# Token tiles ahead of the modulation weights, and a first h made on two engines, at the start of a one-layer diffusion step

## The chip, the cores and the metric

The kernel runs on 1 core of one Trainium2 chip. The metric is the device time of one execution in microseconds (us). In the text PE is TensorE (its matmuls; PEld is its weight loads), DVE is VectorE, ACT is ScalarE, POOL is GpSimd, and SP is SyncE, whose queue issues most DMAs.

## The reference

One trunk layer works on 128 prompt tokens and 1024 sample tokens of width 1024. Cut to what matters here:

```python
shift, scale, gate = modulation(cond, w_mod, b_mod)        # silu(cond) @ w_mod + b_mod, in thirds
h = rmsnorm(x, norm_gain) * (1.0 + scale) + shift           # cond is c_ctx for the prompt, c for the sample
q_a, k_a, v_a, g_a, q_b, k_b, v_b, g_b = split(h @ w_in)    # w_in: 1024 x 2560
# q, k: RMSNorm by head, rotary positions on sample tokens
o_a = global attention of mixer A;  o_b = windowed attention of mixer B with a sink
x = x + gate * (concat(o_a * silu(g_a), o_b * silu(g_b)) @ w_out)
```

The outputs are both new x and the prompt's k and v of both mixers. All is in float32.

## The kernel before, in words

The tokens are 9 tiles of 128 rows: tile 0 is the prompt, tiles 1 to 8 the sample. The width is cut into 8 chunks of 128 (`KT`). A product in float32 is made of three products in a shorter format: each operand is split in a high part (`h_at(0, ...)`, `whi`) and a low part (`h_at(1, ...)`, `wlo`), and high x high, high x low and low x high are summed in PSUM.

The change lies wholly in the first stage, which makes h and, beside it, the gate projection of mixer A (`W_GA`). For each chunk j:

- `load_wm(j)` loads the modulation weights of the chunk (1 MB). `modulate_rows(j)` multiplies them with the conditioning on PE into PSUM tile `pm` and copies the rows out (`mrows`). `modulate(j)` turns these rows on PE, back into `pm`, and DVE sums them (`m4`) into the columns `a_mod` and `b_col`: factor and addend of this chunk.
- `load_x(t)` loads token tile t into `xn`. `norm(t)` takes its sum of squares on ACT, the mean and the power -0.5 on POOL (`msx`, `rsx`), and `scaled` multiplies the tile on DVE.
- `transposed(j, t0, n, cond)` turns n token tiles' chunk j on PE into PSUM tile `px`. ACT makes `hf` = a x px + b from it, DVE casts hf to the high part of h, and POOL subtracts to get the low part.
- `W_GA.split()` makes the high part of the next chunk's weights on ACT and the low part on DVE, and loads one more chunk into one of three buffers `raw`.
- `first_gates` and `next_gates` are the products: `big` for tiles 1 to 4 (512 columns), `small` for tiles 5 and 6 (256 columns), one chunk later.

In pass j of the loop the products of chunk j - 1 run while chunk j is modulated and turned. Passes 0 and 1 have no steady work yet. PE is kept at work there by `warm(n)`: n products of the identity (`ident_b`) into a bank that is overwritten later; their counts stand in `WARM`.

The tiles of PSUM named `pm` and `px` take two banks in turns (`bank_tr`). Each engine executes its instructions in the order of the code, since `in_order` ties them; only semaphores make it wait. The DMAs of SP are issued in that order too, into one queue.

Of the kernel before, what the change touches and what calls it, by code (L numbers as in the profile page):

```python
# [9 lines left out]
F32 = mybir.dt.float32  # L10
F32R = mybir.dt.float32r
BF16 = mybir.dt.bfloat16
AF = mybir.ActivationFunctionType
ALU = mybir.AluOpType
# [4 lines left out]
P = 128  # L19
D = 1024  # L20
KT = D // P
# [34 lines left out]
PAD = 2  # L56
X_FROM = 1
SECOND_FROM = 5
WARM = (8, 4, 4, 2)
WIDE = 5  # L60
LOADLEAD = 5
OUTRATE = 2.5
PADRATE = 3
POOL_LO = ("gb",)
NOG = 5
PES = 3
GATE_LATE = 2
# [40 lines left out]
def hybrid_step(ctx, tc, x_prompt, x_sample, cache_k_a, cache_v_a, cache_k_b, cache_v_b,  # L108
# [3 lines left out]
    nc = tc.nc  # L112
    x_tile = [x_prompt[0]] + [x_sample[0, P * i : P * i + P, :] for i in range(NL)]
# [28 lines left out]
    def bank(tag, name):  # L142
        return ps.tile([P, 512], F32, tag=tag, name=name, bufs=BANKS[tag])
# [5 lines left out]
    def bank_tr(name):  # L149
        turn["tr"] += 1  # L150
        return bank("DE"[turn["tr"] % 2], name)
# [33 lines left out]
    def h_at(lo, i, k, to):  # L185
        c = k - k % GROUP[i]
        return h_tile[lo, i, c][:, k - c, to]


    def third(ts):  # L190

        for i, (a, b) in enumerate(THIRDS):
            if a <= ts.start and ts.stop <= b:
                return i, slice(ts.start - a, ts.stop - a)
# [4 lines left out]
    a_mod = sm.tile([P, KT, 2], F32, name="a_mod")  # L199
    b_col = sm.tile([P, KT, 2], F32, name="b_col")  # L200
# [5 lines left out]
    class Weights:  # L206
# [22 lines left out]
        def split(self):  # L229
            k = len(self.hi)  # L230
            h = wp.tile([P, 512], F32R, tag="whi", name=f"whi{self.tag}_{k}")
            l = wp.tile([P, 512], F32R, tag="wlo", name=f"wlo{self.tag}_{k}")
            nc.scalar.copy(h, self.raw[k])
            eng = nc.gpsimd if self.tag in POOL_LO and k % 2 else nc.vector
            eng.tensor_tensor(l, self.raw[k], h, op=ALU.subtract)
            self.hi.append(h)
            self.lo.append(l)
            self.load()
# [3 lines left out]
    W_GA = Weights([(CG[0], 512)], "ga")  # L242
# [67 lines left out]
    FIRST = [1, 2, 3, 4, 5, 6]  # L310
    with tc.tile_pool(name="st", bufs=2, side="right") as st:
        ident = st.tile([P, P], F32, name="ident", bufs=1)
# [8 lines left out]
        def group_sum(out, eye):  # L321
            nc.vector.tensor_tensor(out, eye[:, 0:2], eye[:, 32:34], op=ALU.add)
            for a in (64, 96):
                nc.vector.tensor_tensor(out, out, eye[:, a : a + 2], op=ALU.add)

        wm = []

        def load_wm(j):
            w = st.tile([P, KT, 2, P], F32, tag="wm", name=f"wm{j}", bufs=3)
            nc.sync.dma_start(w, w_mod_ss[j])  # L330
            wm.append(w)

        load_wm(0)
        nc.scalar.activation(silc, colt[:, 0:16], AF.Silu)
        bsc1 = st.tile([P, 8], F32, name="bsc1", bufs=1)
        st.tile([P, 24], F32, name="pad4", bufs=1)
# [9 lines left out]
        def modulate_rows(j):  # L346
            pm = pmod[j] = bank_tr(f"pm{j}")
            for k in range(KT):
                a = 32 * (k % 4)
                nc.tensor.matmul(pm[a : a + 32, 0:256], sil32[:, k, :], wm[j][:, k].rearrange("p s n -> p (s n)"),  # L350
                                 start=(k < 4), stop=(k >= 4), tile_position=(0, a))
            mrows[j] = st.tile([P, 256], F32, tag="mrows", name=f"mrows{j}")
            (nc.scalar.copy if j else nc.vector.tensor_copy)(mrows[j], pm[:, 0:256])
# [10 lines left out]
                                    op0=ALU.add, op1=ALU.mult)  # L364
            nc.vector.tensor_scalar(b_col[:, j, :], m4[:, 1], colt[:, 24 + j : 25 + j], None, op0=ALU.add)

        xn = {}

        def load_x(t):
            xn[t] = st.tile([P, D], F32, name=f"xn{t}", bufs=1)  # L370
            nc.sync.dma_start(xn[t], x_tile[t])

        rx = {}

        def scaled(t, r):
            nc.vector.tensor_scalar(xn[t], xn[t], r, None, op0=ALU.mult)

        def norm(t, now_=True):
            xm = xn[t]
            sq = st.tile([P, D], BF16, tag="sq", name=f"sq{t}", bufs=1)  # L380
            ss = st.tile([P, 1], F32, tag="ss", name=f"ss{t}")
            nc.scalar.activation(sq, xm, AF.Square, accum_out=ss)
            ms = st.tile([P, 1], F32, tag="ms", name=f"msx{t}")
            nc.gpsimd.tensor_scalar(ms, ss, 1.0 / D, EPS, op0=ALU.mult, op1=ALU.add)
            r = st.tile([P, 1], F32, tag="rs", name=f"rsx{t}")
            nc.gpsimd.tensor_tensor(r, ms, mhalf[:, 0:1], op=ALU.pow)
            if now_:
                scaled(t, r)
            else:
                rx[t] = r  # L390

        def transposed(j, t0, n, cond):
            px = bank_tr(f"px{j}_{t0}")
            for i in range(n):
                if j == 0 and t0 == 1:
                    warm(WARM[3])
                nc.tensor.transpose(px[:, P * i : P * i + P], xn[t0 + i][:, P * j : P * j + P], ident)
            w = P * n
            dst = slice(P * place(t0), P * place(t0) + w)
            hf = st.tile([P, 512], F32, tag="hf", name=f"hf{j}_{t0}", bufs=3)  # L400
            nc.scalar.activation(hf[:, :w], px[:, :w], AF.Identity,
                                 scale=a_mod[:, j, cond : cond + 1], bias=b_col[:, j, cond : cond + 1])
            step = w if third(dst) else 2 * P
            for o in range(0, w, step):
                i, to = third(slice(dst.start + o, dst.start + o + step))
                nc.vector.tensor_copy(h_at(0, i, j, to), hf[:, o : o + step])
                nc.gpsimd.tensor_tensor(h_at(1, i, j, to), hf[:, o : o + step], h_at(0, i, j, to), op=ALU.subtract)

        for t in FIRST[:4]:
            load_x(t)  # L410
        W_GA.load()
        load_x(5)
        load_x(6)
        load_wm(1)
        W_GA.load()
        load_wm(2)
        def warm(n):

            for _ in range(n):
                nc.tensor.matmul(small[0], ident_b, ident_b.unsqueeze(1).to_broadcast([P, 4, P]), start=True, stop=True)  # L420
# [19 lines left out]

        for j in range(KT + 2):
            if j == 0:
                warm(WARM[0])
                norm(1)
                modulate_rows(0)
                warm(WARM[1])
                norm(2)
                modulate(0)
                warm(WARM[2])
                norm(3)  # L450
                norm(4)
                W_GA.split()
                norm(5)
                transposed(0, 1, 4, 0)
                norm(6)
                load_wm(3)
                continue
            big_on, small_on = j <= KT, 2 <= j
            if j < KT:
                W_GA.split()  # L460
            if big_on:
                first_gates(0, j - 1, 0)
                first_gates(1, j - 1, 0)
            if j < KT:
                modulate_rows(j)
                if j + 3 < KT:
                    load_wm(j + 3)
                if X_FROM <= j < X_FROM + 3:
                    load_x(rest[j - X_FROM])
            if big_on:  # L470
                first_gates(0, j - 1, 1)
                first_gates(1, j - 1, 1)
            if j == 1:
                transposed(0, 5, 2, 0)
            if big_on:
                first_gates(2, j - 1)
            if j < KT:
                modulate(j)
                transposed(j, 1, 4, 0)
            if big_on:  # L480
                first_gates(3, j - 1)
            if j < KT:
                transposed(j, 5, 2 if j < WIDE else 4, 0)
            if X_FROM + 1 < j <= X_FROM + 4:
                t = rest[j - X_FROM - 2]
                scaled(t, rx.pop(t))
            if X_FROM < j <= X_FROM + 3:
                norm(rest[j - X_FROM - 1], False)
            for ch in range(4):
                if small_on:  # L490
                    next_gates(ch, j - 2)
                if ch % 2 or j >= KT:
                    more()
            if KT - 2 <= j < KT:
                raw = st.tile([P, KT, 2, P], F32, tag="wm", name=f"raw_qa{j}", bufs=3).rearrange(
                    "p (k a) s n -> p k (a s n)", a=2)
                k0 = 4 * (j - KT + 2)
                c0, n = W_QA.cols[0]
                nc.sync.dma_start(
                    raw, w_in[P * k0 : P * k0 + 512, c0 : c0 + n].rearrange("(k p) n -> p k n", p=P))  # L500
                W_QA.raw += [raw[:, k] for k in range(4)]
# [49 lines left out]
    with tc.tile_pool(name="qt", bufs=2, side="right") as qt:  # L551
# [90 lines left out]
        for m in range(2):  # L642
            w, nxt = ((W_QA, W_QB), (W_QB, W_KV))[m]
            ts = list(range(1, NT)) + [0]
            for t in ts:
# [3 lines left out]
                if (m, t) in ((0, ts[-2]), (1, ts[GATE_AT[0]])):  # L649
                    n = len(wg) // 2  # L650
# [390 lines left out]
    for f in beside[2]:  # L1041
# [5 lines left out]
        name=nc.get_next_instruction_name(), engine=mybir.EngineType.Activation, act_func_set_id=6))  # L1047
# [63 lines left out]
    def values(i, b, last, blk, ph, pl):  # L1111
# [36 lines left out]
        def parts():  # L1148
            while held[0] == NOG:
                outq.pop(0)()  # L1150
# [172 lines left out]
```

## Time and profile before

| | |
|---|---|
| time of 3 runs | 723.15, 723.17, 726.25 us; median 723.17 |
| span of the profiled execution, first to last instruction | 721.3 us |
| mean granted clock of PE over the span | 0.993 |
| busy in the span | PE 97%, DVE 63%, ACT 57%, POOL 46% |
| first real product (first_gates of chunk 0) | starts at 17.47 us |
| modulation products of chunks 1, 2, 3 (`pm`) | start at 18.59, 26.42, 32.72 us |

Of the profiled execution the span is what is known; its own time is not shown apart from it. A row of the timeline gives start, duration, engine, line, operation and tiles (output <- inputs), and in brackets how long the engine stood idle before it and what ended that. Buffer numbers are left out there, so `xn` is any token tile. The granted clock is the share of full speed at which PE may run.

### The profile page before, as it was taken

To read this page: it belongs to the slowest core of one execution; us is meant where nothing else is said; L and a number is where in the kernel's file an instruction comes from. 1 tells how busy PE (TensorE), PEld (TensorE's weight loads), DVE (VectorE), ACT (ScalarE), POOL (GpSimd) and SP (SyncE) were. 2 spreads that over 40 slices of the span, in tenths; PEclk is the share of its full clock that TensorE was granted. 3 is DMA by queue.
4 is the path that set the end of the run, shared out by engine and by line. 5 is a ranking of instruction groups with operands and counts; after the bars stand their busy time and mean duration, and the time that the engine had idled before them with its cause. 6 is when DMAs were issued, how large, how long until landed. Compare 5 with 4: busy or idle time off the path is not lost. (4 is left out here: it accounts for less than half of the span.)

```text
span 721.3 us, 10622 instructions
## 1 busy us (share of the span) xinstructions
PE 698.3 (97%) x3524; PEld 559.7 (78%) x3524; DVE 457.6 (63%) x1007; ACT 411.7 (57%) x829; POOL 335.3 (46%) x355
## 2 busy tenths in 40 slices
PE   5999999999999999999999999999999999999997
PEld 2678988877777788977788888888888888887865
DVE  3466147875675872745866677577666775775653
ACT  5355411411232451158778877877787778877770
POOL 3456013332322340236666555655575557555751
PEclk9999999999999999999999999999999999999999
DMA  8961373348435115440321222121212221212323
GB/s 344 346 219 59 121 278 86 79 94 276 121 85 142 45 60 171 139 143 23 103 67 45 73 67 88 44 81 52 87 54 59 66 87 45 81 53 87 103 65 119
DMA packets 53159, 78.56 MB, mean 109 GB/s; under 512 B 6569, under 2 KB 25449, under 8 KB 52081
## 3 DMA queue, kind: packets, MB, share of 16 engines
q1 hardware_dynamic: 44928, 65.96, 28.1%
q10 hardware_dynamic: 8176, 11.94, 6.3%
q8 instruction: 28, 0.46, 0.3%
q14 instruction: 27, 0.21, 0.1%
HBM read 58.69 MB, written 19.18 MB: 108 GB/s over the span
## 5 line engine op out<-in xcount | busy, mean ns | idle before, releaser
L1108 POOL TENSOR_TENSOR pl<-pe,ph 128x512 fp32r<-128x512 f32 x130 | 167.6, 1292 | 144.7 <-DVE nm L919 67.5
L859 DVE TENSOR_REDUCE mx<-pmx 128x1 f32<-128x384 f32 x192 | 101.4, 552 | 59.5 <-PE pmx L858 58.1
L1100 ACT ACTIVATE pe<-st 128x512 f32<-128x512 f32 x146 | 86.8, 594 | 28.0 <-PE st L1098 27.1
L1104 ACT CAST ph<-pe 128x512 fp32r<-128x512 f32 x146 | 90.6, 621 | 4.8
L1118 PE MATMUL pv<-ph,v_hi 128*128 128x512 f32 x208 | 83.2, 400 | 2.2 <-DVE spare L1142 2.2
L1121 PE MATMUL pv<-pl,v_hi 128*128 128x512 f32 x208 | 82.6, 397 | 0.0
L173 POOL TENSOR_TENSOR rs_q<-ms_q,mhalf 128x8 f32<-128x8 f32 x18 | 34.8, 1931 | 82.1 <-DVE ms_q L171 82.1
L1189 PE MATMUL po<-wo,ogh 128*128 128x512 f32 x216 | 72.5, 394 | 0.2 <-DVE yt L1196 0.2
L919 DVE CUSTOM_DVE_ANT_0 sn<-sn,mask,nsink 128x512 f32<-128x512 f32 (+1 forms) x64 | 46.3, 724 | 38.3 <-PE sn L916 36.5
L858 PE MATMUL pmx<-kha,qt 128*128 128x384 f32 x192 | 61.0, 363 | 0.4 <-ACT pen L905 0.2
L1097 PE MATMUL st<-qt,kha 128*128 128x512 f32 x144 | 58.3, 405 | 1.5 <-ACT pe L1100 0.8
L1098 PE MATMUL st<-qb,kla 68*128 68x512 f32 x144 | 57.6, 400 | 1.1 <-DVE qb L878 1.1
L1120 PE MATMUL pv<-ph,v_lo 128*64 128x512 f32 x146 | 57.9, 396 | 0.0
L1121 PEld LDWEIGHTS pv<-pl,v_hi 128*128 128x128 f32 x208 | 39.4, 189 | 16.7 <-issue 0.2
L905 ACT ACTIVATE pen<-sn,nm 128x512 f32<-128x512 f32 (+2 forms) x72 | 45.0, 626 | 6.5 <-DVE nm L919 3.1
L1093 ACT CAST ph<-st 128x512 fp32r<-128x512 f32 x62 | 36.4, 587 | 19.9 <-PE st L1092 18.7
L1118 PEld LDWEIGHTS pv<-ph,v_hi 128*128 128x128 f32 x208 | 39.4, 189 | 10.5 <-ACT ogh L1154 2.4
L1189 PEld LDWEIGHTS po<-wo,ogh 128*128 128x128 f32 x216 | 40.0, 188 | 6.8 <-DVE yt L1196 0.6
L1094 DVE TENSOR_TENSOR pl<-st,ph 128x512 fp32r<-128x512 f32 x62 | 42.5, 686 | 2.3 <-ACT ph L1093 1.5
L1189 PE MATMUL po<-wo,ogl 128*128 128x512 f32 x108 | 42.6, 394 | 0.0
L594 ACT ACTIVATE sqq<-pq 128x512 f32<-128x512 f32 x18 | 10.8, 599 | 53.3 <-DMA qd<-qo0q 14.4
L858 PEld LDWEIGHTS pmx<-kha,qt 128*128 128x128 f32 x192 | 35.5, 190 | 6.2 <-DVE mx L859 1.4
(216 smaller groups left out, 1700.2 us busy)
## 6 DMA issues: line engine op xcount, KB each, us to landing
qt<-qd SPq DMA_DIRECT2D x36, 256.0 KB, 3.1
wm<-in_w_mod_ss_dram SPq DMA_DIRECT2D x8, 1024.0 KB, 5.1
qd<-qo0q ACTq DMA_DIRECT2D x36, 128.0 KB, 2.4
qd<-qo1q ACTq DMA_DIRECT2D x36, 128.0 KB, 2.4
sgl<-gd SPq DMA_DIRECT2D x36, 128.0 KB, 2.1
out_dram<-yt SPq DMA_DIRECT2D x17, 256.0 KB, 2.1
xn<-in_x_sample_dram SPq DMA_DIRECT2D x8, 512.0 KB, 7.0
wg<-in_w_mod_g_dram SPq DMA_DIRECT2D x4, 1024.0 KB, 7.9
```

What stands on the lines that cost most here:

```text
L858: nc.tensor.matmul(pm[:, 0:384], lhs, kha[:, g, 3 * b : 3 * b + 3, :], start=True, stop=True)
L859: nc.vector.tensor_reduce(mx[:, h, b : b + 1], pm[:, 0:384], axis=AX.X, op=ALU.max)
L919: nc.vector.tensor_tensor_reduce(s, s, mask[:, m0 : m0 + n], -1.0, nsink[:, 4 * g + h : 4 * g + h + 1], op0=ALU.add, op1=ALU.min, accum_ou ...
L1097: nc.tensor.matmul(s, kh, qtile[i], start=True, stop=False)
L1098: nc.tensor.matmul(s, kl, qbtile[i], start=False, stop=True)
L1100: nc.scalar.activation(pe, s, AF.Exp)
L1104: nc.scalar.copy(ph, pe)
L1108: nc.gpsimd.tensor_tensor(pl, pe, ph, op=ALU.subtract)
L1118: nc.tensor.matmul(pv, two, ph, start=(b == 0), stop=False)
L1120: nc.tensor.matmul(pv[0:64, :], vl, ph, start=False, stop=False)
L1121: nc.tensor.matmul(pv, two, pl, start=False, stop=last)
L1189: nc.tensor.matmul(po[n], a, wo_parts[KT * n + k][lo], start=(k == KS[0] and p == 0), stop=(k == KS[-1] and p == 2))
```

## The change

- SP issues the loads of token tiles 1 to 4 ahead of wm0; behind it come the first w_in rows, wm1, the second rows, and only then tiles 5 and 6.
- In pass 0 each tile is turned as soon as it is scaled, with dummy products in between; `modulate_rows(0)` comes ahead of the fourth tile's turn. The dummies are 11, 5, 5, 4, 2 and 7, 34 in all, where 24 were.
- For chunk 0 and tiles 1 to 4, DVE makes hf from px, and ACT makes the high part of h from px too. For all else the old pair stays.
- The low part of the first weights is made on POOL (`POOL_FIRST`).
- Tiles 5 and 6 are normed in pass 1 in place of pass 0, and turned in pass 2 for chunks 0 and 1 at once, into one PSUM tile `px01`.

```diff
-WARM = (8, 4, 4, 2)
+WARM = (11, 5, 5, 4, 2, 7)
...
+POOL_FIRST = (("ga", 0),)
...
-            eng = nc.gpsimd if self.tag in POOL_LO and k % 2 else nc.vector
+            eng = nc.gpsimd if (self.tag in POOL_LO and k % 2) or (self.tag, k) in POOL_FIRST else nc.vector
...
+        for t in FIRST[:4]:
+            load_x(t)
...
-        load_wm(0)
         nc.scalar.activation(silc, colt[:, 0:16], AF.Silu)
...
+        def turned(px, j, t):
+            nc.tensor.transpose(px, xn[t][:, P * j : P * j + P], ident)
...
+        def modulated(px, j, t0, n, cond):
...
+            both = j == 0 and t0 == 1
+            if both:
+                nc.vector.tensor_scalar(hf[:, :w], px[:, :w], a, b, op0=ALU.mult, op1=ALU.add)
+            else:
+                nc.scalar.activation(hf[:, :w], px[:, :w], AF.Identity, scale=a, bias=b)
             for o in range(0, w, step):
                 i, to = third(slice(dst.start + o, dst.start + o + step))
-                nc.vector.tensor_copy(h_at(0, i, j, to), hf[:, o : o + step])
+                if both:
+                    nc.scalar.activation(h_at(0, i, j, to), px[:, o : o + step], AF.Identity, scale=a, bias=b)
+                else:
+                    nc.vector.tensor_copy(h_at(0, i, j, to), hf[:, o : o + step])
                 nc.gpsimd.tensor_tensor(h_at(1, i, j, to), hf[:, o : o + step], h_at(0, i, j, to), op=ALU.subtract)
 
-        for t in FIRST[:4]:
-            load_x(t)
+        load_wm(0)
+        W_GA.load()
+        load_wm(1)
         W_GA.load()
         load_x(5)
         load_x(6)
-        load_wm(1)
-        W_GA.load()
         load_wm(2)
...
             if j == 0:
-                warm(WARM[0])
-                norm(1)
-                modulate_rows(0)
-                warm(WARM[1])
-                norm(2)
-                modulate(0)
-                warm(WARM[2])
-                norm(3)
-                norm(4)
-                W_GA.split()
-                norm(5)
-                transposed(0, 1, 4, 0)
-                norm(6)
-                load_wm(3)
+                px = bank_tr("px0_1")
+                for i in range(4):
+                    norm(1 + i)
+                    warm(WARM[i])
+                    if i == 3:
+                        modulate_rows(0)
+                    turned(px[:, P * i : P * i + P], 0, 1 + i)
+                W_GA.split()
+                warm(WARM[4])
+                modulate(0)
+                modulated(px, 0, 1, 4, 0)
+                warm(WARM[5])
                 continue
...
+            if j == 1:
+                load_wm(3)
+                norm(5, False)
...
-            if j == 1:
-                transposed(0, 5, 2, 0)
+            if j == 2:
+                scaled(6, rx.pop(6))
+                px = bank_tr("px01_5")
+                for i in range(4):
+                    turned(px[:, P * i : P * i + P], i // 2, 5 + i % 2)
+                for i in range(2):
+                    modulated(px[:, 256 * i : 256 * i + 256], i, 5, 2, 0)
...
-            if j < KT:
+            if j == 1:
+                scaled(5, rx.pop(5))
+                norm(6, False)
+            elif j < KT:
                 transposed(j, 5, 2 if j < WIDE else 4, 0)
```

How the rows of three queues change. The number in a name is that of the chunk or tile, and the last one is only a counter. First SP's queue from the first wm or tile on, before:

```order
L330 DMA wm0_169<-in_w_mod_ss_dram 128x2048
L371 DMA xn1_178<-in_x_sample_dram 128x1024
L371 DMA xn2_180<-in_x_sample_dram 128x1024
L371 DMA xn3_182<-in_x_sample_dram 128x1024
L371 DMA xn4_184<-in_x_sample_dram 128x1024
L221 DMA rawga_0_186<-in_w_in_dram 128x512
L371 DMA xn5_188<-in_x_sample_dram 128x1024
L371 DMA xn6_190<-in_x_sample_dram 128x1024
L330 DMA wm1_192<-in_w_mod_ss_dram 128x2048
```

The same place in the changed kernel:

```order
L331 DMA xn1_169<-in_x_sample_dram 128x1024
L331 DMA xn2_171<-in_x_sample_dram 128x1024
L331 DMA xn3_173<-in_x_sample_dram 128x1024
L331 DMA xn4_175<-in_x_sample_dram 128x1024
L339 DMA wm0_184<-in_w_mod_ss_dram 128x2048
L222 DMA rawga_0_186<-in_w_in_dram 128x512
L339 DMA wm1_188<-in_w_mod_ss_dram 128x2048
L222 DMA rawga_1_190<-in_w_in_dram 128x512
L331 DMA xn5_192<-in_x_sample_dram 128x1024
L331 DMA xn6_194<-in_x_sample_dram 128x1024
```

Tiles 1 to 4 moved ahead of wm0, and tiles 5 and 6 behind wm1 and the second rows of w_in.

Second, PE in pass 2, behind the modulation product of chunk 2, before:

```order
L258 MATMUL pg0_0_f_198<-h1_0_1_124,whiga_1_310 128x512
L258 MATMUL pg0_1_f_199<-h1_0_1_124,whiga_1_310 128x512
L262 MATMUL pg0_2_f_200<-h0_0_1_116,whiga_1_310 128x512
L263 MATMUL pg0_2_f_200<-h0_0_1_116,wloga_1_311 128x512
L258 MATMUL pg0_2_f_200<-h1_0_1_124,whiga_1_310 128x512
L359 MATMUL pm2_382<-ident_161,mrows2_391 128x128 x2
L397 MATMUL px2_1_408<-ident_161,xn1_178 128x128
```

The same place in the changed kernel:

```order
L259 MATMUL pg0_0_f_198<-h1_0_1_124,whiga_1_302 128x512
L259 MATMUL pg0_1_f_199<-h1_0_1_124,whiga_1_302 128x512
L395 MATMUL px01_5_395<-ident_161,xn5_192 128x128
L395 MATMUL px01_5_395<-ident_161,xn6_194 128x128
L395 MATMUL px01_5_395<-ident_161,xn5_192 128x128
L395 MATMUL px01_5_395<-ident_161,xn6_194 128x128
L263 MATMUL pg0_2_f_200<-h0_0_1_116,whiga_1_302 128x512
L264 MATMUL pg0_2_f_200<-h0_0_1_116,wloga_1_303 128x512
L259 MATMUL pg0_2_f_200<-h1_0_1_124,whiga_1_302 128x512
L367 MATMUL pm2_377<-ident_161,mrows2_386 128x128 x2
L395 MATMUL px2_1_417<-ident_161,xn1_169 128x128
```

The four turns of tiles 5 and 6 for chunks 0 and 1 now stand ahead of the third column block's products; they stood in pass 1 before. With one PSUM tile less in the turns, px2_1 takes the bank of pm2.

Third, DVE from the cast of chunk 1's h to the sums of chunk 2, before:

```order
L406 CAST h0_0_1_116<-hf1_1_358 128x512
L406 CAST h0_1_0_131<-hf1_5_368 128x256
L235 TENSOR_TENSOR wloga_2_373<-rawga_2_273,whiga_2_372 128x512
L361 TENSOR_REDUCE m4_2_404<-pm2_382 128x4
L363 TENSOR_SCALAR a_mod_148<-m4_2_404,bsc1_172,colt_166 128x2
```

The same place in the changed kernel:

```order
L419 CAST h0_0_1_116<-hf1_1_352 128x512
L378 TENSOR_SCALAR xn5_192<-xn5_192,rsx5_315 128x1024
L236 TENSOR_TENSOR wloga_2_368<-rawga_2_281,whiga_2_367 128x512
L378 TENSOR_SCALAR xn6_194<-xn6_194,rsx6_365 128x1024
L419 CAST h0_1_0_131<-hf0_5_400 128x256
L419 CAST h0_1_0_131<-hf1_5_404 128x256
L369 TENSOR_REDUCE m4_2_413<-pm2_377 128x4
L371 TENSOR_SCALAR a_mod_148<-m4_2_413,bsc1_178,colt_166 128x2
```

The scales of tiles 5 and 6 moved here from pass 0, and the sums of pm2 now stand behind them and behind two casts.

More of the change, by code (lines that the diff above doesn't have):

```diff
@@ L324, in group_sum, with load_x @@
                 nc.vector.tensor_tensor(out, out, eye[:, a : a + 2], op=ALU.add)
+        xn = {}
+        def load_x(t):
+            xn[t] = st.tile([P, D], F32, name=f"xn{t}", bufs=1)
+            nc.sync.dma_start(xn[t], x_tile[t])
+        for t in FIRST[:4]:
+            load_x(t)
         wm = []
@@ L365, in modulate @@
             nc.vector.tensor_scalar(b_col[:, j, :], m4[:, 1], colt[:, 24 + j : 25 + j], None, op0=ALU.add)
[L367 to L371, printed above, removed]
         rx = {}
@@ L394, in transposed @@
             for i in range(n):
-                if j == 0 and t0 == 1:
-                    warm(WARM[3])
-                nc.tensor.transpose(px[:, P * i : P * i + P], xn[t0 + i][:, P * j : P * j + P], ident)
+                turned(px[:, P * i : P * i + P], j, t0 + i)
+            modulated(px, j, t0, n, cond)
+        def modulated(px, j, t0, n, cond):
             w = P * n
@@ L400, in transposed @@
             hf = st.tile([P, 512], F32, tag="hf", name=f"hf{j}_{t0}", bufs=3)
-            nc.scalar.activation(hf[:, :w], px[:, :w], AF.Identity,
-                                 scale=a_mod[:, j, cond : cond + 1], bias=b_col[:, j, cond : cond + 1])
+            a, b = a_mod[:, j, cond : cond + 1], b_col[:, j, cond : cond + 1]
             step = w if third(dst) else 2 * P
+            both = j == 0 and t0 == 1
[3 more added lines that the diff above has]
+                nc.scalar.activation(hf[:, :w], px[:, :w], AF.Identity, scale=a, bias=b)
             for o in range(0, w, step):
                 i, to = third(slice(dst.start + o, dst.start + o + step))
-                nc.vector.tensor_copy(h_at(0, i, j, to), hf[:, o : o + step])
+                if both:
+                    nc.scalar.activation(h_at(0, i, j, to), px[:, o : o + step], AF.Identity, scale=a, bias=b)
+                else:
+                    nc.vector.tensor_copy(h_at(0, i, j, to), hf[:, o : o + step])
                 nc.gpsimd.tensor_tensor(h_at(1, i, j, to), hf[:, o : o + step], h_at(0, i, j, to), op=ALU.subtract)
-        for t in FIRST[:4]:
-            load_x(t)
+        load_wm(0)
+        W_GA.load()
+        load_wm(1)
         W_GA.load()
```

## The prediction

> **What bounds the kernel now.** I read the page first, then the waits of TensorE (PE), then the timeline of the first 40 us, since the diff ends there. The page's first row:
>
> ```profile
> PE 698.3 (97%) x3524; PEld 559.7 (78%) x3524; DVE 457.6 (63%) x1007; ACT 411.7 (57%) x829; POOL 335.3 (46%) x355
> ```
>
> PE is busy in 97% of the span. The idle rest is 23 us, and the change can reach only what lies ahead of and just behind the first real product. In the steady chunks the first projection is bound by PE, so whatever the start gains or loses is carried to the end unchanged. The start, by stretches that I cut at the edges of the clock's changes (columns: stretch, length, busy time of PE, PEld, DVE, ACT, POOL, granted clock, DMA share, GB/s), and the longest waits of PE up to 36 us:
>
> ```profile
> 12.11:15.53 3.42, 2.72 (x15) 1.27 (x12) 2.49 (x7) 2.49 (x5) 2.64 (x6) 1.00 1.04 432
> 15.53:18.94 3.41, 1.61 (x13) 0.93 (x16) 1.45 (x3) 2.43 (x4) 2.12 (x3) 1.00 1.02 423
> 18.94:22.35 3.41, 3.41 (x22) 2.01 (x15) 1.35 (x2) 0.85 (x2) 0.68 (x2) 0.50 1.02 423
> 315.90:319.31 3.41, 2.12 (x9) 1.11 (x8) 1.38 (x4) 3.33 (x7) 1.11 (x1) 1.00 0.74 172
> 319.31:322.72 3.41, 3.31 (x8) 2.21 (x9) 1.37 (x4) 3.35 (x9) 2.60 (x3) 0.50 0.93 302
> PE pg_f L262 <- DVE h L406: 2.2, 2, 1.8
> ```
>
> Two costs stand there. PE waits 1.8 us for the first h. And behind a stretch of 3.41 us in which it worked only 1.61 us, the granted clock is 0.50 for the next 3.41 us, though PE is busy throughout: about 1.7 us of work lost. The same pair stands at 315.9 us, so a half-empty stretch followed by a halved clock is seen twice. The stretch with 2.72 us of work had no drop behind it.
>
> The timeline of the start (start, duration, engine, line):
>
> ```profile
> 2.10 1.99 SPq L371 DMA_DIRECT2D xn<-in_x_sample_dram  x4
> 3.33 3.60 PE L420 MATMUL pg_s<-ident_b 128*128 128x512 bf16 x8 [3.33 <-DVE ident_b L315]
> 6.72 0.33 SPq L330 DMA_DIRECT2D wm<-in_w_mod_ss_dram  x1
> 8.00 1.06 ACT L382 ACTIVATE sq<-xn 128x1024 bf16<-128x1024 f32 x1 [4.51 <-DMA xn<-in_x_sample_dram]
> 9.24 0.19 POOL L384 TENSOR_SCALAR msx<-ss 128x1 f32<-128x1 f32 x1 [6.12 <-ACT sq L382]
> 10.12 0.75 DVE L376 TENSOR_SCALAR xn<-xn,rsx 128x1024 f32<-128x1024 f32 x1 [6.35 <-POOL rsx L386]
> 10.79 0.42 DVE L353 COPY mrows<-pm 128x256 f32<-128x256 f32 x1
> 11.53 1.46 PE L420 MATMUL pg_s<-ident_b 128*128 128x512 bf16 x6
> 11.77 0.33 SPq L330 DMA_DIRECT2D wm<-in_w_mod_ss_dram  x1
> 14.54 0.75 DVE L376 TENSOR_SCALAR xn<-xn,rsx 128x1024 f32<-128x1024 f32 x1 [0.71 <-POOL rsx L386]
> 15.71 0.78 ACT L401 ACTIVATE hf<-px,b_col,a_mod 128x512 f32<-128x512 f32 x1 [0.86 <-PE px L397]
> 16.33 0.75 DVE L376 TENSOR_SCALAR xn<-xn,rsx 128x1024 f32<-128x1024 f32 x1 [0.44 <-POOL rsx L386]
> 17.00 0.42 DVE L406 CAST h<-hf 128x512 fp32r<-128x512 f32 x1
> 17.47 0.50 PE L262 MATMUL pg_f<-h,whiga 128*128 128x512 f32 x1 [1.80 <-DVE h L406]
> 17.50 1.29 POOL L407 TENSOR_TENSOR h<-hf,h 128x512 fp32r<-128x512 f32 x1 [1.20 <-DVE h L406]
> 18.59 1.66 PE L350 MATMUL pm<-wm,sil 128*32 128x256 f32 x16
> ```
>
> The token tiles come last: wm0 is there at 6.72 (the queue's next issue waited for it), tile 4 at 11.77. So the first product hangs on the tiles, and VectorE (DVE) scales tile 5 ahead of the cast of the first h.
>
> And two chunks later, where nothing of the start is felt:
>
> ```profile
> 26.42 1.07 PE L350 MATMUL pm<-wm,sil 128*32 128x256 f32 x16
> 27.56 0.37 ACT L353 COPY mrows<-pm 128x256 f32<-128x256 f32 x1 [1.51 <-PE pm L350]
> 28.69 0.38 PE L359 MATMUL pm<-ident,mrows 128*128 128x128 f32 x2
> 28.91 0.60 PE L397 MATMUL px<-ident,xn 128*128 128x128 f32 x4
> 29.18 0.17 DVE L361 TENSOR_REDUCE m<-pm 128x4 f32<-128x16 f32 x1 [1.81 <-PE pm L359]
> 29.92 1.23 ACT L401 ACTIVATE hf<-px,b_col,a_mod 128x512 f32<-128x512 f32 x2 [1.99 <-DVE b_col L365]
> 30.73 0.75 DVE L406 CAST h<-hf 128x512 fp32r<-128x512 f32 x2 [0.93 <-ACT hf L401]
> 31.69 0.40 PE L262 MATMUL pg_f<-h,whiga 128*128 128x512 f32 x1
> 32.72 1.07 PE L350 MATMUL pm<-wm,sil 128*32 128x256 f32 x16
> 33.41 0.51 POOL L384 TENSOR_SCALAR msx<-ss 128x1 f32<-128x1 f32 x1
> 34.01 0.55 POOL L386 TENSOR_TENSOR rsx<-msx,mhalf 128x1 f32<-128x1 f32 x1
> 37.69 1.79 DVE L376 TENSOR_SCALAR xn<-xn,rsx 128x1024 f32<-128x1024 f32 x1
> ```
>
> A chunk takes 6.30 us (26.42 to 32.72). I compare the two kernels at the third modulation product, pm3, at 32.72 here: by then all that the change moves is done.
>
> **The change part by part.** *Loads.* From 6.72 to 11.77 four tiles land: 1.26 us each, so 2.5 for a wm block of twice the size. With the tiles first, each comes 2.5 us earlier, at about 5.5, 6.7, 8.0 and 9.3; wm0 lands where tile 4 did, at 11.8, the first w_in rows at 12.4, wm1 at 14.9, tiles 5 and 6 at 16.8 and 18.1. The stream stays full, so nothing else is late.
>
> *Norms.* The first scaled tile is done at 10.12 + 0.75 = 10.87 now, at 8.4 then; the next follow in steps of 1.47 (10.12 to 14.54 over three): 9.8, 11.3, 12.8.
>
> *Dummies.* Eleven at 0.43 each (4.1 us from 3.33 at the low clock for ten) end near 8.0, ahead of tile 1, and cost nothing. Two batches of five at 0.22 (1.46 for six with their tail) fit into the steps of 1.47. The batch of four does not: it stands behind tile 3's transpose (11.3 + 0.2) and ahead of pm0, which so starts at 12.4 although wm0 is there at 11.8. Price 0.6 us on the path. The last nine run while DVE and ScalarE (ACT) work: nothing.
>
> *First h.* pm0 at 12.4; 1.14 to its copy (26.42 to 27.56), the copy 0.42, PE turns it at 14.0, and 1.23 later (28.69 to 29.92) a and b are ready: 15.25. Now DVE makes hf from PSUM and ACT makes h from the same PSUM tile. No row shows this DVE operation. The copy of 256 columns takes 0.42 and a four-column operation 0.17, so 512 columns take 0.17 + 2 x 0.25 = 0.67; the bounds are 0.42 (the cast of 512 columns from SBUF) and 0.84 (twice the copy). I take 0.7, the row that reads PSUM. The built program makes ACT's h wait for the DVE count that hf raises, so the two run one after the other: 15.95, then 0.78 on ACT, and the first product at 16.85. That is 0.6 before 17.47. On two engines in this way the step costs 0.7 + 0.78; the old pair would cost 0.78 + 0.43, which is 0.3 less. The low part on POOL starts with the product, as now. Its low part of the first weights also moves to POOL: about 1.3 (the row of 17.50) from 13.0, done long before.
>
> The Trainium skill, "PSUM — Partial Sum Buffer", section "PSUM bank collisions raise a hardware error", says that two engines must not be in one bank at once, reads included, so the second reader has to be held back. By that rule the wait is there for good; no run here shows the two reading together, which would put the forecast 0.7 lower.
>
> *Chunk 1.* At full clock the rows give: first product to pm 1.12 (17.47 to 18.59), pm to the turn 2.27 (26.42 to 28.69), turn to the next h 2.52 (28.69 to 30.73 + 0.43 + 0.05), four products to pm2 1.03 (31.69 to 32.72): 6.94. Now it takes 8.95 (17.47 to 26.42), with the halved clock and the four transposes of tiles 5 and 6. So pm2 comes at 23.8, 2.6 earlier.
>
> *Chunk 2.* It gets the four transposes for both chunks: 0.43, as four start 0.11 apart in the row of 28.91. And two waits that are not in the trace of before.
>
> First, tile 6. ACT squares it behind chunk 1's hf (21.5 + 0.7 = 22.2) and POOL hears of it 1.24 later (8.00 to 9.24): 23.4. POOL is then in h's low part, from 22.8 for 1.29, or up to 1.9 since DVE scales tile 5 at that moment; the row of 37.69, where such a scale took 1.79 in place of 0.75 beside POOL's work, shows that the two hold each other up. Then 0.2 to 0.5 and 0.55 on POOL and 0.75 on DVE: the tile is ready between 25.8 and 26.7. PE is there at 23.8 + 1.0 + 0.57 + 0.2 = 25.6. I take 0.8 of wait (0.2 to 1.1).
>
> Second, chunk 2's own turn. Its px takes the PSUM bank from which DVE still has to read pm2's sums, and in DVE's queue that read now stands behind the two casts of tiles 5 and 6. From tile 6's first transpose: 0.6 to the end of the four, 0.56 and 0.45 on ACT, 0.3 to 0.8 for the second cast, 0.2 for the read: 2.2 to 2.7. PE gets there in 1.45. I take 1.0 (0.75 to 1.25).
>
> Chunk 2 so takes 0.43 + 0.8 + 1.0 = 2.2 more. **Sum:** -2.6 + 2.2 = -0.4 us, between -1.2 and +0.2 by the waits' bounds, some 0.3 more either way by hf and the landings. The profiled execution spans 721.3 us, and the median of the runs shown, 723.17, is 1.87 above that; I keep those 1.87. Forecast: 720.9 + 1.87 = 722.8 us.
>
> **Rivals.** *The halved clock comes back in chunk 2* (slower). The two waits leave PE idle for 1.8 us within 3.5 us near 25.6 to 29, and with the product's wait of about 1 us before. Both drops in the trace stand behind a stretch with 1.3 to 1.8 us idle. If a stretch that decides takes in both waits, the next 3.41 us, full of products, run at half speed: +1.7, 724.5 us. It decides at about 1.5 us idle within one stretch of 3.41; for stretches that could begin anywhere, those which take in enough of both waits are about a third. The Trainium skill, "TensorE: Matmul & The Clock Gate", section "What's actually happening", lets the clock fall only after an idle window of about 3.4 us. By that rule this rival is worth nothing and the time stays 722.8. The length agrees with the trace's 3.41, but the drop at 18.94 came behind 1.61 us of work, so here the measurement decides.
>
> *The first drop stays.* The dummies end near 15.9 and the first product comes at 16.85; if 1 us idle is enough, the 1.7 us remain lost: 724.5 as well. Against it: the stretch with 2.72 of 3.42 us busy drew no drop.
>
> *Chunk 2 has no waits* (faster): POOL takes tile 6's scale ahead of h's low part or DVE reads pm2's sums in time. Then only the 0.43 is added: -2.2, 721.0 us. For it: each wait hangs on a queue order of some tenths. Against it: the rows above give both waits even at their lower bounds.
>
> **How the numbers follow.** Forecast 0.50; clock drop in chunk 2 0.25; first drop stays 0.07; no waits 0.13; something not seen here 0.05. Range 720.8 to 725.2: from the no-wait case to the drop with the upper bounds. About 0.5%, 3.6 us, is what a measurement of this kernel can tell from no change; every case lies inside it, so only what I do not see is left for faster (0.05) and slower (0.05).
>
> **What would show it.** Right: first square near 5.5, pm0 near 12.4, ACT's h starting where DVE's hf ends, first product near 16.9 with the clock at 1.00 behind it, pm2 near 23.8, PE waiting for tile 6's scale and then for pm2's sums, pm3 near 32.3. Wrong: pm3 before 31.2 or after 33.5, hf and h running together, or another clock of 0.50 before 35 us.

## The result

The changed kernel takes 724.37 us (median of 20 runs, 723.48 to 725.65), the kernel before 723.07 (20 runs beside it, 721.69 to 726.25): ratio 1.0017, interval 1.0009 to 1.0025. It is slower by 1.2 us by the ratio, 1.3 by the medians. That lies within 0.5% of no change and within the range forecast, but on the other side of zero: the forecast was a gain of 0.4.

The profiled execution took 725.38 us, span 722.8. First its busy row on the page, then the start by stretches cut at the edges of the clock's changes (columns as before), then PE's waits up to 36 us:

```profile
PE 699.9 (97%) x3534; PEld 560.3 (78%) x3534; DVE 458.2 (63%) x1006; ACT 411.5 (57%) x829; POOL 336.4 (47%) x356
```

```profile
15.71:19.12 3.41, 2.48 (x23) 1.22 (x22) 1.61 (x2) 2.34 (x4) 1.87 (x3) 1.00 1.04 432
19.12:22.53 3.41, 2.65 (x14) 1.91 (x14) 0.84 (x4) 1.43 (x3) 0.29 (x1) 1.00 1.03 420
...
25.95:29.36 3.41, 1.67 (x10) 1.25 (x11) 1.97 (x5) 1.02 (x2) 0.98 (x2) 1.00 1.04 423
29.36:32.77 3.41, 3.41 (x15) 3.02 (x14) 1.29 (x4) 1.62 (x3) 1.71 (x2) 0.50 0.81 330
```

```profile
...
PE px L395 <- DVE m L369: 1.1, 1, 1.1
PE px L395 <- DVE xn L378: 1.0, 2, 0.9
PE pg_f L263 <- DVE h L419: 1.0, 1, 1.0
PE pg_f L263 <- ACT h L417: 0.9, 1, 0.9
```

The wait for the first h has shrunk to 0.9, and the clock stays at 1.00 behind it. In its place stand two new waits of PE in px (0.9 and 1.1), and behind the stretch that holds both the clock is halved. The same in rows of the timeline, with others left out between them:

```profile
5.37 1.06 ACT L384 ACTIVATE sq<-xn 128x1024 bf16<-128x1024 f32 x1 [1.62 <-DMA xn<-in_x_sample_dram]
...
11.91 0.75 DVE L378 TENSOR_SCALAR xn<-xn,rsx 128x1024 f32<-128x1024 f32 x1 [0.71 <-POOL rsx L388]
12.37 1.07 PE L358 MATMUL pm<-wm,sil 128*32 128x256 f32 x16
...
15.13 0.81 DVE L411 TENSOR_SCALAR hf<-px,a_mod,b_col 128x512 f32<-128x512 f32 x1
16.03 0.78 ACT L417 ACTIVATE h<-px,b_col,a_mod 128x512 fp32r<-128x512 f32 x1 [3.09 <-DVE hf L411]
16.86 0.50 PE L263 MATMUL pg_f<-h,whiga 128*128 128x512 f32 x1 [0.93 <-ACT h L417]
...
22.62 0.74 DVE L378 TENSOR_SCALAR xn<-xn,rsx 128x1024 f32<-128x1024 f32 x1
22.78 1.73 POOL L420 TENSOR_TENSOR h<-hf,h 128x512 fp32r<-128x512 f32 x1 [3.37 <-DVE h L419]
23.89 1.07 PE L358 MATMUL pm<-wm,sil 128*32 128x256 f32 x16
24.59 0.52 POOL L386 TENSOR_SCALAR msx<-ss 128x1 f32<-128x1 f32 x1
25.19 0.56 POOL L388 TENSOR_TENSOR rsx<-msx,mhalf 128x1 f32<-128x1 f32 x1
25.46 0.27 PE L395 MATMUL px<-ident,xn 128*128 128x128 f32 x1
25.78 0.75 DVE L378 TENSOR_SCALAR xn<-xn,rsx 128x1024 f32<-128x1024 f32 x1 [0.72 <-POOL rsx L388]
26.59 0.55 PE L395 MATMUL px<-ident,xn 128*128 128x128 f32 x3 [0.86 <-DVE xn L378]
...
27.68 0.38 PE L367 MATMUL pm<-ident,mrows 128*128 128x128 f32 x2
...
28.23 0.79 DVE L419 CAST h<-hf 128x256 fp32r<-128x256 f32 x1 [0.16 <-ACT hf L413]
28.94 0.16 DVE L369 TENSOR_REDUCE m<-pm 128x4 f32<-128x16 f32 x1
29.16 0.97 PE L395 MATMUL px<-ident,xn 128*128 128x128 f32 x4 [1.10 <-DVE m L369]
34.58 1.07 PE L358 MATMUL pm<-wm,sil 128*32 128x256 f32 x16
```

Up to pm2 (23.89, before 26.42) the change gains 2.5 us. By pm3 (34.58, before 32.72) it has lost 4.4 and stands 1.9 behind. Tile 6 is scaled late, since POOL's subtraction (1.73 instead of 1.29, beside DVE's scale of tile 5 and its next split of weights) holds up its msx; then px2_1 waits for DVE's sums of pm2, which stand behind the second cast (28.23, 0.79 long).

One execution misleads here, though. Each timed run also lists its mean granted clock, and both kernels run with and without drops of the clock (a drop is a time in which it is 0.50). One drop of 3.41 us takes 0.0024 off the mean, so 0.999 and above means none. The mean also takes in drops behind PE's last product, like the one from 718.7 us in the profile of before, so the other runs need not all have lost time:

| | runs without a drop | their median | median of all runs | time less span, median of all runs |
|---|---|---|---|---|
| before, first group | 10 of 35 | 721.91 us | 723.20 us | 2.10 us |
| before, second group | 14 of 29 | 721.99 | 722.76 | 2.10 |
| before, third group | 9 of 35 | 722.24 | 723.42 | 2.10 |
| changed, first 20 runs | 7 of 20 | 723.86 | 724.37 | 2.60 |
| changed, again (third group) | 6 of 12 | 723.99 | 724.58 | 2.58 |

The groups are explained below. In the third, where both kernels ran beside each other, the change costs 1.75 us without drops on either side (1.6 to 2.1 over all pairs of these rows); the drops, which cost the kernel before more, hide a part of that.

### The profile page after: what moved, and what is told of

It is laid out like the page before. It is cut to its first block, busy times and chain, and to the rows that moved or that the text cites. A ratio compares the mean times of both kernels' runs of the same rounds, so it can differ in the third digit from the quotient of the medians.

```text
span 722.8 us, 10641 instructions
## 1 busy us (share of the span) xinstructions
PE 699.9 (97%) x3534; PEld 560.3 (78%) x3534; DVE 458.2 (63%) x1006; ACT 411.5 (57%) x829; POOL 336.4 (47%) x356
```

## The experiments

The twelve kernels ran in three groups of four, each group beside its own runs of the kernel before: first fill_waits, early6, early6_px and before_filled; second the three e6px kernels and best; third the other four. Comments in the diffs are added here. Marks are those of each profile: starts of the first product, of pm2 and pm3. The start of the token loads moves by some tenths from execution to execution, so distances between marks compare better than marks.

| kernel | median us (runs) | ratio to before, interval | first | pm2 | pm3 |
|---|---|---|---|---|---|
| changed | 724.37 (20) | 1.0017, 1.0009 to 1.0025 | 16.86 | 23.89 | 34.58 |
| after_again | 724.58 (12) | 1.0016, 1.0006 to 1.0027 | 16.86 | 23.89 | 33.03 |
| fill_waits | 724.29 (12) | 1.0019, 1.0004 to 1.0033 | 16.86 | 23.88 | 33.01 |
| fill_again | 724.51 (12) | 1.0015, 1.0002 to 1.0028 | 16.98 | 24.00 | 33.14 |
| early6 | 723.21 (12) | 0.9998, 0.9988 to 1.0009 | 17.07 | 24.08 | 32.13 |
| early6_px | 721.03 (12) | 0.9972, 0.9959 to 0.9985 | 17.41 | 24.45 | 30.74 |
| tiles56_old | 724.45 (12) | 1.0013, 1.0000 to 1.0027 | 16.85 | 26.43 | 32.72 |
| before | 723.07 (20) | 1 | 17.47 | 26.42 | 32.72 |
| before_filled | 722.13 (12) | 0.9987, 0.9974 to 0.9999 | 17.87 | 25.68 | 31.98 |
| before_loads | 725.39 (12) | 1.0030, 1.0020 to 1.0041 | 20.35 | 28.14 | 34.42 |
| e6px_no4 | 720.73 (12) | 0.9972, 0.9960 to 0.9984 | 16.49 | 23.51 | 29.81 |
| e6px_one | 720.90 (12) | 0.9967, 0.9951 to 0.9982 | 17.05 | 24.07 | 30.36 |
| e6px_no7 | 722.50 (12) | 1.0002, 0.9993 to 1.0010 | 16.93 | 25.48 | 31.78 |
| best | 719.94 (6) | 0.9966, 0.9954 to 0.9979 | 16.00 | 23.01 | 29.30 |

**fill_waits: dummies in both waits of chunk 2**, so that PE works through them and the clock cannot fall there.

```diff
+                    if i == 1:
+                        warm(4)                 # ahead of tile 6's first turn
...
+                if j == 2:
+                    warm(6)                     # ahead of px2_1
```

> The changed kernel with ten more dummy products: four ahead of the turn that waits for tile 6's scale, six ahead of chunk 2's own turn. Both waits of PE in pass 2 stay (0.9 and 1.1 us in the changed kernel's trace), but PE is busy in them. Theory (the waits cost once by themselves and once more by the halved clock that follows them): no clock of 0.50 near 29 us, pm3 near 32.9 in place of 34.58, time some 1.4 us below the changed kernel's 724.4, about 723.0. Rival (only the waits cost, the clock drop is not caused by them): a drop stays, pm3 near 34.6, time 724.4.

```profile
25.56 1.03 PE L432 MATMUL pg_s<-ident_b 128*128 128x512 bf16 x4
26.59 0.55 PE L395 MATMUL px<-ident,xn 128*128 128x128 f32 x3
...
27.89 1.46 PE L432 MATMUL pg_s<-ident_b 128*128 128x512 bf16 x6
29.19 0.62 PE L395 MATMUL px<-ident,xn 128*128 128x128 f32 x4
...
33.01 1.07 PE L358 MATMUL pm<-wm,sil 128*32 128x256 f32 x16
```

The timeline of this kernel: the dummies fill the waits, px starts at 26.59 and 29.19 (26.59 and 29.16 without them), and the clock holds. So the drop was worth 34.58 - 33.01 = 1.57 in that one execution, as the theory had it. But the timed median is no lower (724.29 against 724.37), as the rival had it, so this drop is not what makes the change slow. **fill_again** repeats it in the third group, beside **after_again**, the changed kernel once more.

> The changed kernel with four and six dummies in pass 2's two waits, once more. Theory: PE's work hides the idle time from the clock, so more runs than of the changed kernel show the full clock, these near 723.9; the waits themselves stay. Rival: the share of runs below the full clock and their times are those of the changed kernel.

> The changed kernel once more, to have its runs beside the next one's on one chip. Theory (a halved clock behind pass 2's waits, in that part of the executions whose stretches of 3.41 us take in both waits): runs without any drop near 723.9, runs with one in pass 2 some 1.5 higher, so that the upper third lies near 725. Rival (no such drop in the timed runs): all runs near 724 at any clock.

They are alike again (724.51 and 724.58), and six of twelve runs of each are without a drop, so the dummies did not raise that share. The profile of after_again has the same waits, but pm3 at 33.03 with no early drop. Its stretch (between the steps of the clock counted on from 9.03 us, where this execution reached full speed) takes in less of the first wait:

```profile
26.09:29.50 3.41, 1.80 (x11) 1.39 (x12) 1.97 (x5) 1.02 (x2) 1.11 (x2) 1.00 1.04 423
```

Idle for 1.61 of 3.41 us, it drew no drop; idle for 1.74, the stretch from 25.95 in the first profile did.

**early6: tile 6 normed, and tiles 5 and 6 scaled, earlier in pass 1**, the turns still in pass 2.

```diff
+                if j == 1:                      # pass 1, behind load_x
+                    scaled(5, rx.pop(5))
+                    norm(6, False)
...
+                if j == 1:                      # behind modulate(1)
+                    scaled(6, rx.pop(6))
...
-                scaled(6, rx.pop(6))            # pass 2
...
-            if j == 1:                          # end of pass 1
-                scaled(5, rx.pop(5))
-                norm(6, False)
...
```

> The changed kernel with tile 6's square sum moved ahead of chunk 1's h on ACT and the scales of tiles 5 and 6 moved into pass 1's free time on DVE; the turn of both tiles stays in pass 2. Theory: PE's wait for tile 6's scale (0.9 us) is gone, the wait for the sums of pm2 behind two casts stays (1.1 us); about 1.2 us idle in one stretch is too little for a drop, so pm3 near 31.7, time near 722. Rival (one wait of 1.1 us is enough to halve the clock): pm3 near 33.3, time 723.4.

**early6_px: the same, and px01 turned at the end of pass 1** instead of in pass 2.

> As the one with tile 6's sum early, and the four turns of tiles 5 and 6 for chunks 0 and 1 at the end of pass 1, where PE waits for chunk 1's h in the changed kernel. Theory: both waits of pass 2 and the drop are gone, pm3 near 29.9, which is 2.8 us before the kernel before's 32.72; time near 720.6, faster than both. Rival (what comes after pm3 is not bound by PE and takes the gain back): pm3 near 29.9 and the time still at 722 or more.

The waits of PE up to 36 us, in early6 for tiles and sums, then in early6_px:

```profile
PE px L395 <- DVE m L369: 1.1, 1, 1.1
...
PE px L395 <- DVE xn L378: 0.3, 1, 0.3
```

```profile
PE px L395 <- DVE xn L378: 2.0, 4, 0.8
PE pg_f L263 <- ACT h L417: 0.9, 1, 0.9
```

In early6 the wait for tile 6 is gone (the 0.3 on a tile lies ahead of the first product) and the one for the sums is left. From first product to pm3 it is 15.06 us, where fill_waits has 16.15: 1.09 less, and the timed median is 1.08 lower. That is 1.2 above the 722 expected; no drop followed the wait of 1.1 in this profile, and some 0.5 of it would be the time outside the span, which is 2.6 here as in the changed kernel. In early6_px the wait for the sums is gone too; three of the four waits for a tile lie ahead of the first product, the fourth (0.43) ahead of tile 6's turn, in a gap in which PE would have waited for the cast of h. From first product to pm3 it is 13.33, another 1.73 less: about the second wait, and the 0.43 that the four turns cost in chunk 2. The timed median is 2.18 lower, since the time outside its span is 0.36 shorter as well. The waits were thus taken away one after the other, and the change without them is faster than the kernel before by 0.28% (0.15 to 0.41%).

**tiles56_old: only the handling of tiles 5 and 6 as before** (normed and scaled at the start of pass 1, chunk 0 turned in pass 1, chunk 1 behind it), with all else changed.

```diff
-                norm(5, False)
+                norm(5)
+                norm(6)
...
+            if j == 1:
+                transposed(0, 5, 2, 0)
```

> The changed kernel with tiles 5 and 6 treated the old way: both normed at the start of pass 1 and scaled at once, turned in pass 1 for chunk 0 and chunk 1 apart. Their loads stay late (16.8 and 18.1). Theory (the late load of these two tiles is what makes PE wait, wherever they are turned): the wait moves to pass 1, about 2.5 us there, pm2 near 26.4, pm3 near 32.6, so time near 723.2, no better than before. Rival (the turn for two chunks at once is the whole loss): pm3 near 30.6, time near 721.3.

```profile
20.32 0.30 PE L395 MATMUL px<-ident,xn 128*128 128x128 f32 x1 [0.59 <-DVE xn L378]
21.70 0.33 PE L395 MATMUL px<-ident,xn 128*128 128x128 f32 x1 [1.08 <-DVE xn L378]
```

Chunk 2 takes 6.29 again, but chunk 1 takes 9.58, because PE now meets the late tiles earlier (timeline of this kernel). The time stays (724.45). So the loss does not belong to turning two chunks at once: tiles 5 and 6 arrive later in the new load order. With early6 and early6_px it follows that their scales should go early on DVE and their turns to where PE would wait anyway.

**before_filled: the kernel before with `warm(8)` behind `transposed(0, 1, 4, 0)`**, so that PE works through its wait for the first h.

> The kernel before with one edit: eight dummy products behind the fourth tile's turn, where PE waits 1.8 us for the first h. Theory (the first halved clock follows from this idle time): no clock of 0.50 near 19 us, first product at 17.5 as before, pm2 near 25.1 in place of 26.42, pm3 near 31.4, time near 721.9. Rival (the drop comes whatever PE does there, or costs nothing since others bound pass 1): pm2 near 26.4, time 723.1.

Chunk 1 takes 7.81 us (17.87 to 25.68) where the profile of before has 8.95, and the clock holds until 318.5. The time falls by 0.13% (0.01 to 0.26%) to 722.13; its seven runs without a drop have a median of 722.02, as the kernel before has without one (721.91). A gain from removing that drop is there in a part of the runs only.

**before_loads: the kernel before with the new load order only.**

> The kernel before with the new order of loads alone: tiles 1 to 4 ahead of wm0, tiles 5 and 6 behind wm1 and the second w_in rows. Theory (the new loads need the new order of work: ACT squares and DVE scales tile 5 ahead of the first h, and it now lands at 16.8): first product near 19.8 in place of 17.5, pm3 near 33.6, time near 723.5 to 724.5, slower. Rival (the loads are what gains): first product earlier than 17.5, time below 722.5.

The waits of PE in this kernel, and two rows of DVE in its timeline:

```profile
PE pm L357 <- DMA wm<-in_w_mod_ss_dram: 4.7, 1, 4.7
```

```profile
13.71 0.42 DVE L360 COPY mrows<-pm 128x256 f32<-128x256 f32 x1 [5.54 <-PE pm L357]
14.05 0.74 DVE L377 TENSOR_SCALAR xn<-xn,rsx 128x1024 f32<-128x1024 f32 x1
```

Alone the order loses (1.0030), and more than the 723.5 to 724.5 expected. The old pass 0 has the copy of wm0's rows ahead of tile 2's scale on DVE, so that scale, ready long before, stands behind PE's wait for wm0. PE, idle until then, also takes 1.94 us for pm0, where the changed kernel takes 1.07. The first product comes at 20.35. The loads gain only with the rewritten pass 0.

**Three parts of pass 0, each taken out of early6_px.** e6px_no4 has no dummies ahead of `modulate_rows(0)`, e6px_one makes the first h on ACT and DVE as before, e6px_no7 has no dummies under the first h.

```diff
-WARM = (11, 5, 5, 4, 2, 7)
+WARM = (11, 5, 5, 0, 2, 7)                      # e6px_no4
+WARM = (11, 5, 5, 4, 2, 0)                      # e6px_no7
...
-            both = j == 0 and t0 == 1
+            both = False                        # e6px_one
```

> The one with both waits of pass 2 gone (tile 6's sum early, the turn at the end of pass 1), without the four dummy products that stand behind tile 3's turn and ahead of pm0. Theory (they stand on the path to the first h, since wm0 is there at 11.8): pm0 starts when wm0 has landed, some 0.7 us earlier against tile 3's scale, the first product too; time near 720.3 in place of 721.0. Rival (PE's idle time there halves the clock, or another wait takes their place): first product no earlier, time 721 or more.

> The one with both waits of pass 2 gone, but with the first h made the old way: hf on ACT, its cast on DVE. Theory (in the changed way the two engines run one after the other, 0.81 + 0.78 us, against 0.78 + 0.43): from b to the first product 0.3 us less, time near 720.7. Rival (two engines save time): first product later by up to 0.4, time near 721.4.

> The one with both waits of pass 2 gone, without the last seven dummy products, so that PE stands idle some 2.6 us ahead of the first product. Nothing else waits for these dummies. Theory (a stretch of 3.41 us with over 1.5 us idle halves the clock for the next one): a clock of 0.50 near 18 to 21 us in nearly every execution, first product as before, pm2 some 1.5 us later, time near 722.4. Rival (the clock falls only behind a stretch without any work): no drop, time 721.0.

From tile 3's scale to the first product it is 5.92 us without the four dummies and 6.42 with them: they cost 0.5. The first h in e6px_one:

```profile
15.44 0.22 DVE L373 TENSOR_SCALAR b_col<-m,colt 128x2 f32<-128x2 f32 x1
15.76 0.78 ACT L413 ACTIVATE hf<-px,b_col,a_mod 128x512 f32<-128x512 f32 x1 [1.99 <-DVE b_col L373]
16.57 0.43 DVE L419 CAST h<-hf 128x512 fp32r<-128x512 f32 x1 [0.91 <-ACT hf L413]
17.05 0.50 PE L263 MATMUL pg_f<-h,whiga 128*128 128x512 f32 x1 [0.54 <-DVE h L419]
```

From b_col to the product it takes 1.61, against 1.99 in early6_px with both engines on px: the old pair is 0.38 faster. Neither gain can be told from zero in the times (720.73 and 720.90, in another group than 721.03). The seven dummies are different:

```profile
10.55:13.96 3.41, 3.35 (x28) 1.22 (x25) 1.84 (x3) 0.67 (x2) 1.95 (x3) 1.00 1.00 414
13.96:17.37 3.41, 0.97 (x6) 0.59 (x5) 1.44 (x5) 1.27 (x3) 0.90 (x2) 1.00 1.05 426
17.37:20.79 3.42, 3.42 (x21) 1.39 (x20) 2.12 (x2) 1.26 (x4) 1.73 (x3) 0.50 1.02 418
```

Without them (e6px_no7, stretches) PE works 0.97 of 3.41 us and the clock is halved behind it. None of its 12 runs reaches a mean clock of 0.999, and the time rises to 722.50. So these seven are worth about 1.5 us (1.47 against early6_px, 1.60 against e6px_one of the same group), and they are what takes the old drop away.

**best: early6_px without the four dummies, with the old pair for the first h, and `warm(3)` ahead of px01 in pass 1.**

> All that the runs so far point to: tile 6's sum early, the turn of tiles 5 and 6 at the end of pass 1, no four dummies ahead of pm0, the first h made the old way, and three dummies where PE waits for tile 6 at the end of pass 1. Theory: the gains add up to some 1.0 us on top of the one with both waits gone, first product near 15.9 to 16.3, time near 720.0, faster than both kernels. Rival (the path to the first h then ends at tile 4's scale, or the later stages take it back): time 721.

719.94 us, ratio 0.9966 (0.9954 to 0.9979): faster than both kernels, than the one before by 2.5 us.

## Why the prediction was wrong

**Up to pm2 each step held in the profile.** Square at 5.37 (forecast 5.5), pm0 at 12.37 (12.4), hf and h one after the other in 0.81 and 0.78 (0.7 and 0.78), first product at 16.86 (16.85), chunk 1 in 7.03 (6.94), pm2 at 23.89 (23.8). The price of the four dummies was 0.5 (0.6), the loss by using both engines 0.38 (0.3). That the first product came within 0.01 us is partly luck: a and b were ready 0.12 earlier than forecast, and hf took 0.11 longer. The Trainium skill, "PSUM — Partial Sum Buffer", section "PSUM bank collisions raise a hardware error", has two engines kept out of one bank at a time. The trace agrees: h starts 0.09 behind the end of hf.

Three terms of the sum failed behind that; the sum below gives the share of each.

**The base.** The gain at pm2 was reckoned against the one execution in the trace, with its drop at 18.94 us taken as a property of the kernel. A third of the runs of before (33 of 99) have no drop anywhere, and in those that part of the gain is not to be had. Without the drop, pm3 of before comes at about 31.6 (31.98 in before_filled, whose first product is 0.4 later), not at 32.72. So the -2.6 at pm2 is about -1.5 in an execution without drops; the other 1.1 can be gained only where the drop is.

**Chunk 2's extra was mis-sized**: 2.2 forecast, 33.01 - 23.88 - 6.30 = 2.83 measured in fill_waits, with the clock at 1.00. Both waits are there, with the releasers that the text named, at 0.86 (0.8) and 1.10 (1.0). But an idle time is not its whole price. From tile 5's turn to tile 6's it takes 1.13 where two turns stand 0.11 apart; from the turn of pm2 to px2_1 1.48 where it takes 0.22 (28.69 to 28.91 before). The waits so cost 1.02 and 1.26, 0.5 more than forecast. That they are what slows chunk 2 is shown by early6 and early6_px, which are without them.

**The time outside the span was kept at 1.87.** It is 2.10 before and 2.60 after (2.03 to 2.23 and 2.53 to 2.66 over all runs of the two). That is another 0.5 us, and nothing in the trace of before told of it. What causes it is open.

**The sum by these measurements**, taken from the third group: without drops the span goes from 720.1 to 721.4 (+1.3; pm3 at 33.0 less 31.6 gives 1.4); outside it +0.5; the drops cost the median run of before 1.2 (723.42 less 722.24) and that of the changed kernel 0.6 (724.58 less 723.99), -0.6. Together +1.2, as measured there (724.58 less 723.42). In the same terms the forecast was +0.7 without drops (-2.6 + 1.1 + 2.2), 0 outside the span, and -1.1 for the drop, counted in full: -0.4. Of the miss of 1.6 us, 0.6 is thus chunk 2's extra, 0.5 the time outside the span, and 0.5 the drop.

**The rival with the halved clock in chunk 2** happened in the profiled execution, in the place and at nearly the price given (1.57; forecast 1.7), and pm3 so came after the text's bound of 33.5. It is not the cause of the slower median, as fill_waits shows; that its 724.5 us lies near the result is luck. Nor did the 1.5 us of idle time at which it was to set in follow from the rows shown: the stretch from 315.90 was idle for 1.29 us and drew a drop. "The first drop stays" and "no waits" did not occur in the profiles of the changed kernel.

## What to carry to other kernels

Before a gain is reckoned against a trace, ask whether the stall in it happens in every execution: times and clocks of many runs tell, and one profile doesn't. When a load is moved back, follow what hangs on it through each queue: here two scales and a read, each some tenths late, cost more than the earlier tiles won, and moving the scales forward and the turns back made the change a gain. A wait of an engine in a full pipeline can cost more than its idle time, here 0.16 us more for each of the two, and is read from the distance between starts.

## What the runs showed of the hardware

- The clock was halved behind stretches of 3.41 us in which PE worked 0.97, 1.61, 1.67 and 2.12 us, and not behind 2.48, 2.65 and 2.72, but also not behind the 1.80 of after_again or the 1.65 of before_filled (7.93 to 11.34 us). So the busy time of the trace does not decide alone: the limit that the prediction took, 1.5 us idle, is too simple, and what else counts is open. The Trainium skill, "TensorE: Matmul & The Clock Gate", section "What's actually happening", lets the clock fall after an idle window of about 3.4 us. The length agrees; that the window must be idle does not.
- The stretches don't start with the program: the clock's record begins, at 1.00, between 6.3 and 9.4 us in the thirteen profiles other than before_loads, where PE stood idle early and it begins at 16.0. So whether a wait of 1 to 2 us costs a drop changes from run to run. With a gap of 2.4 in 3.41 (e6px_no7) none of 12 runs had a mean clock of 0.999.
- A halved stretch of 3.41 us that begins near 319 us costs less than the 1.1 and 1.57 us of those at the start. Without a drop, pm3 to the span's end takes 688.2 us (fill_waits); with one of 3.41 us near 320, 688.9 (fill_again), and with one of 6.8 us, 690.1 (after_again).
- The time outside the span belongs to the build: 2.1 us for before, before_filled and before_loads, 2.6 for the changed kernel, fill_waits, early6 and tiles56_old, 2.2 for early6_px and those made from it. Neither the load order nor the dummies set it, since before_loads has 2.1 and fill_waits 2.6. What does is open.
- DVE and POOL hold each other up also here: POOL's subtraction took 1.29 alone (before, at 17.50) and 1.73 and 1.84 beside DVE's work (changed kernel, at 22.78; early6, at 22.98). In the changed kernel at 17.35 it was DVE that took longer, 1.38 for the split of weights that took 0.69 in before at 20.40.
